# Low key parts with half zeros: a 128-row second score matmul in a decoder trunk on one core

## The chip, the core and the metric

The kernel runs on one core of one Trainium2 chip. The metric is the device time of one execution in microseconds (us): the median of several runs. Five engines of the core appear below: TensorE (PE, with its weight loads as PEld), VectorE (DVE), ScalarE (ACT), GpSimd (POOL) and SyncE (SP), which issues most DMAs.

## The reference

Two layers of a decoder trunk on 512 tokens of width 1024: a norm, one input projection, two attention branches (differential attention with rotary embedding; stick-breaking attention), projections merged under sigmoid gates, an output projection, then a gated FFN of 2816. The change touches the scores alone, which both branches compute per head of 64 features:

```python
def probs(qb, k):                      # differential attention, two maps per head
    sc = jnp.einsum('bhqd,bhkd->bhqk', qb, k).astype(jnp.float32) * scale
    sc = jnp.where(mask, sc, -jnp.inf)
    return jax.nn.softmax(sc, axis=-1)
...
z = jnp.einsum('bhqd,bhkd->bhqk', qb, k).astype(jnp.float32) * scale   # stick-breaking
log_beta = jax.nn.log_sigmoid(z)
log_rem = jnp.where(mask, jax.nn.log_sigmoid(-z), 0.0)
after = lax.cumsum(log_rem, axis=key_axis, reverse=True) - log_rem
a = jnp.where(mask, jnp.exp(log_beta + after), 0.0)
```

## The kernel before

Everything lies with features on partitions. A float32 value is held as a high part in a rounded format (fp32r) and a low part, the rest; a product is high x high, high x low and low x high, in three passes of TensorE. Weights come in chunks of 128x1024 by SyncE's queue, are split by ScalarE (L111) and VectorE or GpSimd (L113), and feed 8 times three matmuls of 128x512 (L204 to L206).

A layer's attention is cut into 8 units: four pairs of stick-breaking heads ("s"), then four differential heads ("d"). A unit has two score maps, c = 0 and 1, each of 64 features: rows 0 to 63 and 64 to 127 of the unit's q and k. A map's scores are cut by query block of 128 tokens, and since later keys are masked, block by block 128, 256, 384 or 512 keys are computed (`SEG`). With heads of 64 features, two of the three passes fit one matmul: `stack_k` lays the high part of a key into both halves of a 128-row tile (`ka`, `kb`), `stack_q` lays high and low part of the query into the two halves (`qa`, `qb`), and one 128-row matmul does high x high and low x high (L397). The third pass, query high times key low, is a matmul of 64 rows: `kl` holds the low parts of both keys, one in each half, and the matmul takes the half of its map from `kl` and from the query tile (L398). There are 2 layers x 16 maps x 4 blocks = 128 of these.

After a map's scores come, for "s", two sigmoids (ACT L427, L429), a mask (POOL L433), a scan (DVE L435) and a product (POOL L437), for "d" a masked softmax (L473 to L489); then transposes on TensorE (L411), the split of their result (ACT L414, DVE L415) and the product with the values (L448, L449 for "s", L504 to L506 for "d"). `LAG` puts two maps between the scores and the product; projections of the next units and of the gates fill TensorE in between (`FILL`).

The program is written unit by unit; a scheduler then sets each engine's order from its own estimate of times. Tiles come from pools: tag `stk` has 8 buffers in turn for `ka`, `kb`, `kl`, `qa`, `qb`, and a new tile of a tag waits until the old one in its buffer has been read. Later gates take `stk` buffers too (`gate_group`). Engines work through their own queue in order, so a waiting instruction holds up those behind it.

Of the kernel before, what the change touches and what calls it, by code (L numbers as in the profile page):

```python
# [24 lines left out]

# score segments of a head: query block -> (bank, column in bank, column in SBUF, keys)
SEG = {0: (0, 0, 0, 128), 2: (0, 128, 128, 384), 3: (1, 0, 512, 512), 1: (2, 0, 1024, 256)}
BANKS = ((0, 512), (512, 512), (1024, 256))
# transposed probabilities: key block -> (bank, column in bank, column in SBUF)
TSEG = {0: (0, 0, 0), 1: (1, 0, 512), 3: (1, 384, 896), 2: (2, 0, 1024)}  # L30
# columns of the packed parameters
C_NA, C_NF, C_NL, C_BG, C_SL, C_LP = 0, 16, 32, 40, 72, 74

# buffers per tag, in the attention pools and of PSUM banks
BUFS = dict(mx=4, sm=4, blk=12, tmp=5, stk=8, v=3, wk=4, wT=3)
BANK_BUFS = dict(mm=3, at=5)
W_BUFS, W_AHEAD = 4, 2
GATES_IN_BLK = 4
FILL = (3, 3, 3, 3, 4, 4, 4, 4)  # projection groups issued under each pair of score maps
LAG = 2  # maps between the scores of a map and its product with the values  # L40


def f32(ap):
    return ap.bitcast(F32)
# [3 lines left out]
def trunk(ctx: ExitStack, tc, xT, par, tab, scn, msk, w_in, w_o, w_out, w_fi, w_fo, out):  # L48
# [9 lines left out]

# [1 line left out]
    UNITS = [("s", i) for i in range(4)] + [("d", i) for i in range(4)]  # L60
# [35 lines left out]
    def w_pieces(*steps):  # L96
        """Loads the next weight chunk and splits it, piece by piece."""
        n = state["next"]
        state["next"] = n + 1
        src = w_src(stream[n])  # L100
        cols = src.shape[1]
        raw = wp.tile([P, 1024], F32, name=f"wr{n}", tag="wr", bufs=2)
        hi = wp.tile([P, 1024], F32R, name=f"wh{n}", tag="wh", bufs=W_BUFS)
        lo = wp.tile([P, 1024], F32R, name=f"wl{n}", tag="wl", bufs=W_BUFS)
        ready.append((stream[n], hi, lo))
        at = 0
        for n_cols in steps:
            c = slice(at, min(at + n_cols, cols))
            at = c.stop
            nc.sync.dma_start(out=raw[:, c], in_=src[:, c])  # L110
            nc.scalar.copy(out=hi[:, c], in_=raw[:, c])  # L111
            eng = nc.gpsimd if stream[n][1] == "in" and n % 4 == 0 else nc.vector
            eng.tensor_tensor(out=lo[:, c], in0=raw[:, c], in1=f32(hi[:, c]), op=ALU.subtract)  # L113
            yield
# [11 lines left out]

# [1 line left out]
    pt = cst.tile([P, C_LP], F32, name="pt")  # L128
# [9 lines left out]

    # the array's clock comes up while the first loads are under way
    warm = bank("mm", "warm")  # L140
    for i in range(9):
        nc.tensor.matmul(warm[:, :P], ones_d, ones_d, start=True, stop=True)

# [1 line left out]
    xs = []  # L145
# [3 lines left out]
    def rsqrt_of(make, ms, name):  # L149
        """1/sqrt(ms + eps) over a PSUM bank: exp(-ln/2), then a Newton step."""  # L150
        y, t = make(f"y{name}"), make(f"t{name}")
        nc.scalar.activation(out=y, in_=ms, func=AF.Ln, bias=eps[:, 0:1])
        state["exp"] = nc.scalar.activation(out=y, in_=y, func=AF.Exp, scale=-0.5)
        nc.vector.scalar_tensor_tensor(out=t, in0=y, scalar=-0.5, in1=y, op0=ALU.mult, op1=ALU.mult)
        nc.vector.scalar_tensor_tensor(out=t, in0=ms, scalar=EPS, in1=t, op0=ALU.add, op1=ALU.mult)
        nc.vector.scalar_tensor_tensor(out=y, in0=t, scalar=1.5, in1=y, op0=ALU.add, op1=ALU.mult)
        return y

    class Norm:
        """Collects a norm as the tiles of x arrive: x*g in two parts, and the mean square."""  # L160

# [32 lines left out]
    def mm(dst, key, rhs, first=True, last=True):  # L194
        """dst += W^T rhs over the k tiles of one weight chunk, three exact passes each."""
        hi, lo = w_get(*key)
        mm_tiles(dst, hi, lo, rhs, first, last)
# [10 lines left out]
    def table(name, after=None):  # L208
        """Loads an activation table set once the work that needs the one before is issued."""
        if after is None:  # L210
            return nc.scalar.preload_act_table_set(name)
        with tc.issue_after(after.ins):
            return nc.scalar.preload_act_table_set(name)
# [25 lines left out]
    for l in range(DEPTH):  # L239
        nc.vector.tensor_tensor(out=lpp[:, l], in0=lpt[:, l, :, 0], in1=lpt[:, l, :, 1], op=ALU.mult)  # L240
        nc.vector.tensor_reduce(out=lps[:, l], in_=lpp[:, l], axis=AX.X, op=ALU.add)
        nc.scalar.activation(out=lps[:, l], in_=lps[:, l], func=AF.Exp)
        li = 0.8 - 0.6 * math.exp(-0.3 * l)
        # the negated weight of the second map
        nc.vector.scalar_tensor_tensor(out=lam[:, l:l + 1], in0=lps[:, l, 1:2], scalar=-li,
                                       in1=lps[:, l, 0:1], op0=ALU.add, op1=ALU.subtract)
        nc.vector.tensor_scalar(out=gsub[:, l:l + 1], in0=pt[:, C_SL + l:C_SL + l + 1],
                                scalar1=1.0 - li, scalar2=None, op0=ALU.mult)
# [14 lines left out]
    for l in range(DEPTH):  # L263
        h = nrm.h
        with ExitStack() as ac:
# [22 lines left out]
            nc.vector.tensor_tensor(out=cs[:, 1], in0=cs[:, 1], in1=r, op=ALU.mult)  # L288

            gates = {}  # L290
            pair = [None]
            TAIL = list(TAIL0)

            def gate_group(key):
# [4 lines left out]
                if n < GATES_IN_BLK:  # L299
                    t = blk(f"gt{j}")  # L300
                elif n < GATES_IN_BLK + BUFS["stk"]:
                    t = T("stk", f"gt{j}")
                else:
                    q = (n - GATES_IN_BLK - BUFS["stk"]) % 2
                    if q == 0:
                        pair[0] = T("wk", f"gt{j}", (P, 1280))
                    t = pair[0][:, q * S:q * S + S]
# [3 lines left out]
            class Unit:  # L311
                """A pair of score maps: two stick-breaking heads, or the two maps of a diff head."""

# [38 lines left out]
                def stack_k(self, t):  # L352
                    ka, kb, kl = self.stk("ka"), self.stk("kb"), self.stk("kl")
                    nc.scalar.copy(out=ka[0:64], in_=t[0:64])
                    nc.scalar.copy(out=kb[64:128], in_=t[64:128])
                    nc.vector.tensor_copy(out=ka[64:128], in_=t[0:64])
                    nc.vector.tensor_copy(out=kb[0:64], in_=t[64:128])
                    nc.vector.tensor_tensor(out=kl[0:64], in0=t[0:64], in1=f32(ka[0:64]), op=ALU.subtract)
                    nc.vector.tensor_tensor(out=kl[64:128], in0=t[64:128], in1=f32(kb[64:128]), op=ALU.subtract)
                    self.k = (ka, kb, kl)  # L360
# [27 lines left out]
                def scores(self, c):  # L388
                    ka, kl = self.k[c], self.k[2]
                    qs = self.q[c]  # L390
                    hs = slice(c * 64, c * 64 + 64)
                    bs = [bank("at", f"s{self.n}{c}{i}_{l}") for i in range(3)]
                    for qb in (0, 2, 3, 1):
# [3 lines left out]
                        nc.tensor.matmul(dst, qs[:, qc], ka[:, 0:n], start=True, stop=False)  # L397
                        nc.tensor.matmul(dst, qs[hs, qc], kl[hs, 0:n], start=False, stop=True)  # L398
                    return bs

                def transposed(self, w, name):
                    """w (queries on partitions) -> its two parts with keys on partitions."""
                    bs = [bank("at", f"t{name}{i}_{l}") for i in range(3)]
# [15 lines left out]
            class SB(Unit):  # L419
                def maps(self, c):  # L420
                    name = f"{self.n}{c}"
                    bs = self.scores(c)
                    # a[k] = beta[k] * prod of (1 - beta[j]) over k < j < q, beta = sigmoid(score / 8)
                    e = T("wk", "e" + name, (P, 1280))
# [6 lines left out]
                    for o in (0, 384, 896, 1152):  # L431
                        d = z[:, o:o + P]
                        nc.gpsimd.tensor_tensor(out=d, in0=d, in1=mk[:, 1], op=ALU.mult)  # L433
                    # masked keys hold the product at one, which also starts each segment afresh
                    nc.vector.tensor_tensor_scan(out=e[:, ::-1], data0=e[:, ::-1], data1=msc[:, ::-1], initial=1.0,  # L435
# [126 lines left out]

# [1 line left out]
            def parts(t, hi, lo):  # L564
# [37 lines left out]
        with ExitStack() as fc:  # L602
# [31 lines left out]
            if last:  # L634
                # the last tile by halves of the tokens: the first half is normed and stored under the second
                w7 = [w_get(l, "fo", 7, c) for c in range(3)]
# [21 lines left out]

# [1 line left out]
def _tiles(np, w, kt, nt):  # L660
    """(L, kt*128, nt*128) -> (L, nt, 128, kt*128): one output tile's weights together."""
    L = w.shape[0]
# [49 lines left out]
```

## Time and profile before

| | |
|---|---|
| median of 3 runs | 1550.02 us (1549.92 to 1557.08) |
| profiled execution, first to last instruction | 1546.8 us |
| the rest of it, by the median | 3.2 us |
| PE busy | 1519.6 us (98%), 6756 matmuls |
| PEld busy | 1229.7 us |
| DVE / ACT / POOL busy | 868.5 / 613.6 / 401.2 us |
| layer 0, attention | about 20 to 300 us |
| layer 1, attention | about 767 to 1080 us |

A busy time adds up the durations of an engine's instructions, and matmuls overlap one another, so PE at 98% does not say that it is at its peak. The chain that ended last is followed back from the last instruction to whatever released each step: it tells where a shorter time would shorten the end. A granted clock of 1.00 is TensorE's 2.4 GHz level, 0.50 its 1.2 GHz level.

### The profile page before, as it was taken

The page shows a single profiled execution, that of the slowest core. Times are in us where ns is not written, and L with a number is a line of the kernel's source. Part 1 is how long each engine was busy: PE and PEld are TensorE (multiplying, and loading weights), DVE is VectorE, ACT ScalarE, POOL GpSimd, SP SyncE. Part 2 cuts the span into 40 slices and gives each one's busy share as a digit, 9 for nine tenths or more (in the row PEclk, how much of TensorE's full clock was granted, in tenths as well). Part 3 has the DMA queues.
Part 4 walks back from the last instruction along what each step waited for, and adds up shares of the span by engine and source line. Part 5 has one row for each costly group of instructions (what it writes and reads, how often), then busy time and mean ns, then how long its engine had stood idle before and what let it go on. Part 6 is the DMA issues. An engine that isn't in the chain of part 4 may idle for free.

```text
span 1546.8 us, 17367 instructions
## 1 busy us (share of the span) xinstructions
PE 1519.6 (98%) x6756; PEld 1229.7 (79%) x6756; DVE 868.5 (56%) x1070; ACT 613.6 (40%) x968; POOL 401.2 (26%) x280
## 2 busy tenths in 40 slices
PE   8999999999999999999998999999999999999997
PEld 6777777888888888888876777778888888888886
DVE  5978867575544545433366778664755444544223
ACT  5655454453422222322254545535433322223221
POOL 3777543001111111100147755410011111111011
PEclk9999999999999999999998989999999999999999
DMA  6122232233323232333321222322322323233331
GB/s 209 65 69 75 69 101 70 82 96 96 96 95 97 95 105 93 95 99 90 119 69 55 61 60 85 96 68 69 109 96 95 96 96 101 94 105 90 98 96 59
DMA packets 43618, 139.58 MB, mean 90 GB/s; under 512 B 5648, under 2 KB 8080, under 8 KB 43536
## 3 DMA queue, kind: packets, MB, share of 16 engines
q1 hardware_dynamic: 42240, 137.38, 28.4%
q8 instruction: 53, 0.87, 0.2%
q10 hardware_dynamic: 1296, 1.09, 0.2%
q14 instruction: 29, 0.24, 0.0%
HBM read 132.16 MB, written 2.10 MB: 87 GB/s over the span
## 4 chain that ended last, share of the span: by engine, by line
PE 88%; DVE 5%; issue 2%; ACT 2%; POOL 1%; DMA 1%; SPq 1%; DVEq 0%; POOLq 0%; ACTq 0%
PE fg L204 5%; PE fu L204 5%; PE fg L205 5%; PE fu L205 5%; PE fu L206 5%; PE fg L206 5%; PE fo L204 5%; PE fo L206 5%; PE fo L205 5%; PE pg L204 4%; PE pg L205 4%; PE pg L206 4%; PE pd L204 2%; PE pd L205 2%; PE pd L206 2%; PE wo L205 2%
## 5 line engine op out<-in xcount | busy, mean ns | idle before, releaser
L111 ACT CAST wh<-wr 128x1024 fp32r<-128x1024 f32 (+3 forms) x251 | 258.0, 1029 | 627.0 <-PE fu L206 160.8
L113 DVE TENSOR_TENSOR wl<-wr,wh 128x1024 fp32r<-128x1024 f32 (+2 forms) x229 | 325.9, 1424 | 205.2 <-ACT wh L111 204.9
L617 POOL TENSOR_TENSOR u<-u,g 128x512 f32<-128x512 f32 x44 | 56.8, 1292 | 441.5 <-DVE u L616 394.3
L205 PE MATMUL fo<-ah,wl 128*128 128x512 f32 (+1 forms) x374 | 141.0, 377 | 0.0
L204 PE MATMUL fo<-ah,wh 128*128 128x512 f32 (+1 forms) x374 | 141.0, 377 | 0.0
L206 PE MATMUL fo<-al,wh 128*128 128x512 f32 (+1 forms) x374 | 140.8, 376 | 0.0
L204 PE MATMUL fg<-hhf,wh 128*128 128x512 f32 x352 | 137.7, 391 | 0.0
L206 PE MATMUL fu<-hlf,wh 128*128 128x512 f32 x352 | 136.9, 389 | 0.0
L205 PE MATMUL fg<-hhf,wl 128*128 128x512 f32 x352 | 136.9, 389 | 0.0
L206 PE MATMUL fg<-hlf,wh 128*128 128x512 f32 x352 | 136.9, 389 | 0.0
L204 PE MATMUL fu<-hhf,wh 128*128 128x512 f32 x352 | 136.9, 389 | 0.0
L205 PE MATMUL fu<-hhf,wl 128*128 128x512 f32 x352 | 136.9, 389 | 0.0
L616 DVE TENSOR_TENSOR u<-fu,yf 128x512 f32<-128x512 f32 x44 | 30.4, 691 | 129.5 <-PE fu L206 129.5
L204 PE MATMUL pg<-hha,wh 128*128 128x512 f32 x256 | 101.6, 397 | 0.0
L205 PE MATMUL pg<-hha,wl 128*128 128x512 f32 x256 | 100.7, 393 | 0.0
L206 PE MATMUL pg<-hla,wh 128*128 128x512 f32 x256 | 100.7, 393 | 0.0
L205 PEld LDWEIGHTS fo<-ah,wl 128*128 128x128 f32 x374 | 70.4, 188 | 13.1
L206 PEld LDWEIGHTS fo<-al,wh 128*128 128x128 f32 x374 | 70.4, 188 | 12.9
L204 PEld LDWEIGHTS fo<-ah,wh 128*128 128x128 f32 x374 | 70.4, 188 | 12.7
L113 POOL TENSOR_TENSOR wl<-wr,wh 128x1024 fp32r<-128x1024 f32 (+3 forms) x22 | 48.7, 2212 | 114.4 <-ACT wh L111 93.1
L204 PE MATMUL pd<-hha,wh 128*128 128x512 f32 x192 | 78.2, 408 | 0.0
L205 PE MATMUL pd<-hha,wl 128*128 128x512 f32 x192 | 78.1, 407 | 0.0
(265 smaller groups left out, 3133.6 us busy)
## 6 DMA issues: line engine op xcount, KB each, us to landing
wr<-in_w_fi_dram SPq DMA_DIRECT2D x88, 512.0 KB, 3.5
wr<-in_w_in_dram SPq DMA_DIRECT2D x78, 512.0 KB, 3.6
wr<-in_w_fo_dram SPq DMA_DIRECT2D x32, 512.0 KB, 3.6
wr<-in_w_o_dram SPq DMA_DIRECT2D x16, 512.0 KB, 3.5
wr<-in_w_out_dram SPq DMA_DIRECT2D x16, 512.0 KB, 3.5
wr<-in_w_fo_dram SPq DMA_DIRECT2D x16, 384.0 KB, 3.2
x<-in_xT_dram SPq DMA_DIRECT2D x8, 256.0 KB, 5.5
cs<-in_tab_dram SPq DMA_DIRECT2D x2, 512.0 KB, 5.3
```

Source lines behind the costliest of these rows:

```text
L111: nc.scalar.copy(out=hi[:, c], in_=raw[:, c])
L113: eng.tensor_tensor(out=lo[:, c], in0=raw[:, c], in1=f32(hi[:, c]), op=ALU.subtract)
L204: nc.tensor.matmul(dst, hi[:, c], rh, start=first and k == 0, stop=False)
L205: nc.tensor.matmul(dst, lo[:, c], rh, start=False, stop=False)
L206: nc.tensor.matmul(dst, hi[:, c], rl, start=False, stop=last and k == n - 1)
L616: nc.vector.tensor_tensor(out=u, in0=bu, in1=r, op=ALU.mult)
L617: nc.gpsimd.tensor_tensor(out=u, in0=u, in1=g, op=ALU.mult)
```

## The change

The low parts of the two keys of a unit get a tile of 128 rows each, `klz[set][c]`. Map 0's low part lies in rows 0 to 63 of the one, map 1's in rows 64 to 127 of the other, and the other half of each is zero. The second score matmul then takes the whole query tile and the whole `klz` tile: the rows that hold the query's low part meet zeros. Four such tiles (two sets, taken in turn by units) are made per layer, and GpSimd writes the zero halves once per layer. `stk` goes from 8 to 6 buffers, and two of the later gates take the tiles of set 0. Comments and blank lines aside, this is all:

```diff
-BUFS = dict(mx=4, sm=4, blk=12, tmp=5, stk=8, v=3, wk=4, wT=3)
+BUFS = dict(mx=4, sm=4, blk=12, tmp=5, stk=6, v=3, wk=4, wT=3)
...
+            klz = [[T(f"klz{b}{c}", f"klz{b}{c}", dt=F32R) for c in range(2)] for b in range(2)]
+            for b in range(2):
+                for c in range(2):
+                    nc.gpsimd.memset(f32(klz[b][c])[64 - 64 * c:128 - 64 * c], 0.0)
...
                 elif n < GATES_IN_BLK + BUFS["stk"]:
                     t = T("stk", f"gt{j}")
+                elif n < GATES_IN_BLK + BUFS["stk"] + 2:
+                    t = T(f"klz0{n - GATES_IN_BLK - BUFS['stk']}", f"gt{j}")
...
                 def stack_k(self, t):
-                    ka, kb, kl = self.stk("ka"), self.stk("kb"), self.stk("kl")
+                    ka, kb = self.stk("ka"), self.stk("kb")
+                    kl = klz[UNITS.index((self.kind, self.i)) % 2]
...
-                    nc.vector.tensor_tensor(out=kl[0:64], in0=t[0:64], in1=f32(ka[0:64]), op=ALU.subtract)
-                    nc.vector.tensor_tensor(out=kl[64:128], in0=t[64:128], in1=f32(kb[64:128]), op=ALU.subtract)
+                    nc.vector.tensor_tensor(out=kl[0][0:64], in0=t[0:64], in1=f32(ka[0:64]), op=ALU.subtract)
+                    nc.vector.tensor_tensor(out=kl[1][64:128], in0=t[64:128], in1=f32(kb[64:128]), op=ALU.subtract)
...
                 def scores(self, c):
-                    ka, kl = self.k[c], self.k[2]
+                    ka, kl = self.k[c], self.k[2][c]
                     qs = self.q[c]
-                    hs = slice(c * 64, c * 64 + 64)
...
                         nc.tensor.matmul(dst, qs[:, qc], ka[:, 0:n], start=True, stop=False)
-                        nc.tensor.matmul(dst, qs[hs, qc], kl[hs, 0:n], start=False, stop=True)
+                        nc.tensor.matmul(dst, qs[:, qc], kl[:, 0:n], start=False, stop=True)
```

Lines behind the new ones carry higher numbers in the changed kernel: the score matmuls are L405 and L406 there, the transposes L419, the products with the values L456 and L457.

In layer 1 the order is kept. TensorE at the scores of its last unit, before (`sd` is the score bank, `kad` and `kbd` the high parts, `kld` the low parts):

```order
L397 MATMUL sd_1_7689<-kad_1_7471,qad_1_7522 128x128
L398 MATMUL sd_1_7689<-kld_1_7473,qad_1_7522 128x128
L397 MATMUL sd_1_7689<-kad_1_7471,qad_1_7522 128x384
L398 MATMUL sd_1_7689<-kld_1_7473,qad_1_7522 128x384
L397 MATMUL sd_1_7690<-kad_1_7471,qad_1_7522 128x512
```

And the same place after:

```order
L405 MATMUL sd_1_7689<-kad_1_7472,qad_1_7522 128x128
L406 MATMUL sd_1_7689<-klz_1_5869,qad_1_7522 128x128
L405 MATMUL sd_1_7689<-kad_1_7472,qad_1_7522 128x384
L406 MATMUL sd_1_7689<-klz_1_5869,qad_1_7522 128x384
L405 MATMUL sd_1_7690<-kad_1_7472,qad_1_7522 128x512
```

Nothing moved there; only the low part comes from a tile of its own.

In layer 0 the order of all engines differs. TensorE at the first product with the values of that layer, before (`ts` are the transposes of the first map, `avs_0_615` its product with the values: `ths` the high, `tls` the low part):

```order
L411 MATMUL ts_0_595<-ident,zs_0_365 128x128 x4
L411 MATMUL ts_0_596<-ident,zs_0_365 128x128 x2
L448 MATMUL avs_0_615<-ths_0_597,vs_0_348 128x512
L397 MATMUL ss_0_666<-kbs_0_412,qbs_0_454 128x128
L449 MATMUL avs_0_615<-tls_0_598,vs_0_348 128x512
L398 MATMUL ss_0_666<-kls_0_413,qbs_0_454 128x128
```

And after:

```order
L419 MATMUL ts_0_601<-ident,zs_0_372 128x128 x2
L204 MATMUL ps_0_796<-hha_124,wh_634 128x512
...
L456 MATMUL avs_0_620<-ths_0_602,vs_0_355 128x512
L405 MATMUL ss_0_671<-kbs_0_419,qbs_0_460 128x128
L406 MATMUL ss_0_671<-klz_0_325,qbs_0_460 128x128
L405 MATMUL ss_0_671<-kbs_0_419,qbs_0_460 128x384
L457 MATMUL avs_0_620<-tls_0_603,vs_0_355 128x512
```

Three projection matmuls (`ps`) and two more score matmuls now stand between the last transposes and the product that needs the low part `tls`.

GpSimd at the start of layer 0, after (`acca` is the sum of squares of the norm, `wl` the low part of a weight chunk, `qas` the query tile of the first unit):

```order
L187 TENSOR_TENSOR acca_102<-acca_102,sqa_183 128x512
L294 MEMSET klz_0_322 64x512
L294 MEMSET klz_0_323 64x512
L294 MEMSET klz_0_324 64x512
L294 MEMSET klz_0_325 64x512
L113 TENSOR_TENSOR wl_229<-wr_227,wh_228 128x1024
L113 TENSOR_TENSOR wl_561<-wr_559,wh_560 128x1024
L375 TENSOR_TENSOR qas_0_342<-qns_0_340,qas_0_342 64x512
```

Before, the weight split stood right behind the sum of squares; the four memsets have come between the two.

## Rows read from the trace of the kernel before

**Rows 1.** The page's chain that ended last, share by engine.

```profile
PE 88%; DVE 5%; issue 2%; ACT 2%; POOL 1%; DMA 1%; SPq 1%; DVEq 0%; POOLq 0%; ACTq 0%
```

**Rows 2.** Timeline of TensorE, layer 0: start us, duration us, line, tiles, rows*columns, form.

```profile
216.09 0.38 PE L398 MATMUL sd<-kld,qad 64*128 64x256 f32 x1
216.40 0.33 PE L397 MATMUL sd<-kbd,qbd 128*128 128x128 f32 x1
216.66 0.33 PE L398 MATMUL sd<-kld,qbd 64*128 64x128 f32 x1
216.91 0.44 PE L397 MATMUL sd<-kbd,qbd 128*128 128x384 f32 x1
217.28 0.44 PE L398 MATMUL sd<-kld,qbd 64*128 64x384 f32 x1
217.65 0.50 PE L204 MATMUL pd<-hha,wh 128*128 128x512 f32 x1
```

**Rows 3.** Timeline of TensorE, layer 1, a product with the values, all rows full.

```profile
1010.78 0.33 PE L504 MATMUL avd<-thd,vd 128*128 128x384 f32 x1
1010.95 0.34 PE L505 MATMUL avd<-tld,vd 128*128 128x384 f32 x1
...
1011.43 0.28 PE L505 MATMUL avd<-tld,vd 128*128 128x256 f32 x1
1011.54 0.29 PE L506 MATMUL avd<-thd,vd 128*128 128x256 f32 x1
...
1011.73 0.28 PE L505 MATMUL avd<-tld,vd 128*128 128x128 f32 x1
1011.84 0.27 PE L506 MATMUL avd<-thd,vd 128*128 128x128 f32 x1
```

**Rows 4.** L398 by stretch: length, busy (xcount) of PE and PEld, clock, DMA.

```profile
40.00:78.50 38.50, 4.66 (x12) 2.12 (x12) 0.96 0.17 55
108.60:137.50 28.90, 4.15 (x10) 1.77 (x10) 1.00 0.25 73
137.50:300.00 162.50, 13.47 (x33) 6.03 (x33) 1.00 0.25 79
780.70:830.90 50.20, 4.83 (x14) 2.30 (x14) 0.99 0.23 74
887.20:926.60 39.40, 4.02 (x8) 1.77 (x8) 0.87 0.18 54
926.60:1080.00 153.40, 11.69 (x28) 5.22 (x28) 0.98 0.26 81
```

**Rows 5.** Chain's shares from 62.7, 108.6, 780.7 and 887.2 us on, as the text says.

```profile
by line: DVE es L435 46.2%; issue 16.3%; DVE wl L113 11.7%; DVE kas L356 5.4%; DVE kls L358 5.3%; DVE vs L384 4.7%; DVE tls L415 3.9%; DVE kbs L357 3.6%; DVE qns L321 3.0%; DVE kls L359 0.2%
...
by line: DVE es L435 23.2%; issue 17.0%; DMA knd0s<-knd0u 6.9%; POOL zs L433 6.4%; POOL knd L334 6.2%; POOL knd0u L329 6.1%; SPq L333 6.1%; DVE kld L359 5.8%; DVE tls L415 4.8%; ACT es L427 4.8%; ACT zs L429 3.4%; DVE kad L356 2.4%; DVE kbd
...
by line: issue 12.8%; POOL zs L433 10.4%; DVE kls L359 10.4%; DMA wr<-in_w_in_dram 8.8%; ACT wh L111 8.2%; DVE wl L113 7.7%; DVE kls L358 6.6%; DVE kas L356 5.0%; POOL zs L437 4.8%; POOL qbs L367 4.3%; POOL qas L366 2.6%; ACT qas L364 2.5%;
...
by line: issue 14.3%; DMA qnd0s<-qnd0u 9.5%; DVE wl L113 9.4%; SPq L333 8.9%; DMA knd1s<-knd1u 8.2%; DVE kld L358 6.6%; DVE kbd L357 6.4%; DVE kld L359 4.3%; DVE tls L415 4.2%; DVE qnd L330 3.9%; ACT ths L414 3.4%; POOL knd L334 3.3%; POOL 
```

**Rows 6.** Stretches: length, busy of PE, PEld, DVE, ACT, POOL, then clock, DMA.

```profile
830.00:840.00 10.00, 9.05 (x22) 6.56 (x23) 6.69 (x8) 4.43 (x9) 6.97 (x6) 0.50 0.18 52
...
1021.20:1024.60 3.40, 3.40 (x8) 2.26 (x9) 2.29 (x7) 0.00 (x0) 0.00 (x0) 0.50 0.47 154
983.70:987.00 3.30, 3.30 (x9) 2.53 (x10) 3.30 (x10) 1.64 (x7) 0.47 (x1) 0.50 0.50 164
```

**Rows 7.** Timeline of TensorE, two waits, in brackets: idle us before, released by.

```profile
78.51 0.50 PE L449 MATMUL avs<-tls,vs 128*128 128x512 f32 x1 [1.15 <-DVE tls L415]
...
830.95 0.79 PE L449 MATMUL avs<-tls,vs 128*128 128x512 f32 x1 [4.40 <-DVE tls L415]
```

**Rows 8.** GpSimd: a memset in the groups by line; a row of its timeline.

```profile
masks.py:197 POOL MEMSET ident<- 128x128 f32 x1 | 0.2, 204 | 0.3 <-POOLq L703 0.3
...
28.64 2.39 POOL L113 TENSOR_TENSOR wl<-wr,wh 128x1024 fp32r<-128x1024 f32 x1 [5.88 <-ACT wh L111]
```

## The prediction

> **What bounds the kernel now.** I read the chain that ended last first: 88% of the span is TensorE, 5% VectorE, everything else 7% [rows 1]. So a microsecond taken from TensorE is worth a microsecond wherever the chain lies on it, and nothing where it does not. The second view is the timeline of TensorE inside a score map, where the change works. The reader should look at starts, not at durations: matmuls overlap, and the time that one takes of the engine is the distance from its start to the next start. In a run of projections and scores of layer 0 [rows 2] the start after the 64-row matmul of 256 columns comes 0.31 us later (216.09 to 216.40), after that of 128 columns 0.25, after that of 384 columns 0.37. The full-row matmuls between them are as slow: 0.26 for 128 columns, 0.37 for 384. Full-row matmuls of the same widths that follow one another, in the product with the values, take 0.17 us for 384 columns, 0.11 for 256 and 0.11 for 128 [rows 3]. They add into one bank just as the score pair does, so it is not the accumulation that costs. What is left is that the number of rows of the array changes, from 128 to 64 or back, and each change costs 0.14 to 0.20 us whatever the width.
>
> Third, the granted clock: in 1021.20 to 1024.60 it is 0.50, the 1.2 GHz level, right behind a stretch of nothing but such scores, and in 830.00 to 840.00 it is 0.50 behind a long wait of TensorE [rows 6].
>
> **The change part by part.**
>
> *Row changes removed.* There are 2 layers x 16 maps x 4 query blocks = 128 low-part matmuls. Two changes of 0.14 to 0.20 us on each, 0.36 us together at the mean of rows 2, would be 46 us. That is too much, since the first change of a run, behind an ordinary projection, is cheaper (about 0.1 us), and some low-part matmuls stand next to each other. I therefore took the same difference over the whole timeline, for each pair of neighbouring matmuls whose row counts differ (248 pairs were recorded, five of them in rows 2): distance of the starts, less the distance that full-row matmuls of that width have. It comes to 40.0 us, 0.31 per low-part matmul. The streamed columns stay as they are: the second matmul reads as many columns as before, half of its rows being zero. So 40.0 us of engine time goes.
>
> *What of it lies on the path.* In four stretches the chain leaves TensorE for 12 us or more at a time [rows 5]: 62.7 to 78.5 (46.2% of it the scan), 108.6 to 137.5, 780.7 to 830.9 and 887.2 to 926.6. There TensorE waits for VectorE, GpSimd or a shuffle by DMA, and arriving earlier only makes it wait longer. I also count the scores from 40 us on as lost, since behind them the same VectorE queue ends at 78.5. By the counts of low-part matmuls [rows 4] 12 + 10 + 14 + 8 = 44 of them lie there: 44 x 0.31 = 13.6 us lost. What is on the path is 40.0 - 13.6 = 26.4 us.
>
> *Clock.* The half-clock stretch of 1021.20 to 1024.60 costs about 1.7 us (half of 3.4), and one of the same length at 983.7 follows the same kind of stretch [rows 6]. Behind neither did the engine wait for data; only the row changes had thinned its work. I take both as gone: 3.4 us. Against that stands the wait at 78.51: today 1.15 us, it would grow by 12 x 0.31 = 3.7 to 4.9, longer than the 4.40 us at 830.95 [rows 7], and that one was followed by 10 us at 0.50, which cost 5 us. I give that an even chance: 2.5 us back. Sum: 26.4 + 3.4 - 2.5 = 27.3 us.
>
> *Zero halves.* Four GpSimd memsets of 64x512 per layer. No row shows one of this size; one of 128x128 takes 0.2 us, and a two-operand operation on 1024 columns takes 2.39 us [rows 8], so half of that, 1.2 us, bounds one of 512 columns from above. Four take 0.8 to 4.8 us. The order puts them in layer 0 between the last sum of squares and a weight split that waits 5.88 us for its data today [rows 8], and in layer 1 just as far ahead of the units, where GpSimd waits long. They are covered: 0. If the cover failed, or VectorE's splits beside them were slowed, 0 to 2 us in layer 0; that goes into the range.
>
> *Key stacking.* The two subtractions write two tiles instead of two halves of one, with the same shape: 0. *Two stack buffers fewer:* a unit now takes four buffers of six instead of five of eight. Counting the rotation through, each k tile still reuses a q or low tile of the unit two before, and each q tile a k tile of the unit before, so no wait is added; the low parts alternate between two sets, again two units apart. The gates find the same number of places. All 0.
>
> *Order.* In layer 1 all engines keep their order but for the memsets. In layer 0 the scheduler has moved projections, scores and the products with the values against each other. TensorE's first product with a low part (the wait at 78.51) now has three projections, a product and three scores between it and the last transposes, where a product and one score stood; elsewhere such a cover shrinks by as much. I take 0 with 5 us to either side, the size of the largest wait of rows 7.
>
> **The rivals.** *The other engines eat more of it.* If VectorE's queue ends every map of the stick-breaking half, only the scores from 137.5 to 300 and from 926.6 to 1080 count: 33 + 28 = 61 [rows 4], 61 x 0.31 = 18.9, less 2.5 for the clock: 1533.6 us. For it: in both layers the chain leaves TensorE early in that half. Against it: in 78.5 to 108.6 and 830.9 to 887.2 it is TensorE again.
>
> *All of it arrives.* The waits shrink with their inputs, since the chains through VectorE begin at a score: 40.0 + 3.4 = 43.4, so 1506.6 us. Against it: the stretch from 780.7 begins at the norm, not at a score.
>
> *The gap stays.* It is 0.14 to 0.20 us long, and one weight load is 0.18 us (2.12 us for 12 in rows 4). Were it a weight load that could not run under the matmul before, full-row scores would pay it too: 1550, with up to 2 us of memsets 1552. Against it stand rows 3: there full-row loads are hidden, at 0.17 us for 384 columns. The Trainium skill, on the page "TensorE: Matmul & The Clock Gate", Part 3, says that a weight load overlaps a running matmul only where the row groups differ; by that rule the new pair, both on all rows, would keep the gap and the time would be this rival's. The trace does not agree: the 0.17 us of rows 3 leave no room for a load of 0.18 us beside the streaming.
>
> *Slower.* The new order of layer 0 puts a consumer on TensorE's queue too early, as at 830.95: such a place costs 4.40 us of wait and 5 us of half clock, 9.4 together. It decides from three such places on (28 us); with four the time is 1550.0 - 27.3 + 37.6 = 1560.3 us. Against it: the distances from a map's scores to its transposes, counted in matmuls, are much as they were in either layer.
>
> **How the numbers follow.** The profiled execution's span is 1546.8 us, 3.2 under the median 1550.02 of the timed runs; I take the 3.2 as unchanged. 1550.0 - 27.3 = 1522.7, so 1523 us. Chances: the forecast 0.60, other engines eat more 0.18, all of it 0.12, the gap stays 0.05, slower 0.05. The range leaves out the last two and reaches from all of it, 1507, to the first rival with the order against it, 1533.6 + 5, with the memsets 1540. 0.5% of the time, about what a measurement of this kernel can tell from no change, is 7.8 us. Faster by more than that: 0.60 + 0.18 + 0.12 = 0.90. Within it: 0.05. Slower: 0.05.
>
> **What would show it.** In the profile after, the low-part matmuls should read 128*128, and within a map the starts should lie 0.11, 0.11 to 0.13, 0.17 and 0.23 us apart; a 128-column pair still 0.25 apart would show the third rival. Layer 1, where the order did not change, is the clean place: from 926.6 to 1080 it should get shorter by 28 x 0.31 + 3.4 = 12 us, while 780.7 to 830.9 should hardly move and its waits grow by 4 us. The clock should be full behind the last scores of layer 1. If the wait at 78.51 does not grow, the first stretch was not bound as I read it, and more of the 13.6 us arrives; if layer 0 gains much less than layer 1, the new order is the place to look.

## The result, and the profile after

The changed kernel takes 1536.49 us (median of 4 runs, 1535.02 to 1538.29), the kernel before beside it 1551.79 (4 runs, 1549.92 to 1557.08). The ratio is 0.9889, with a 95% interval of 0.9862 to 0.9916: 17 us faster by the ratio (15 by the two medians), where 27 were forecast. The time lies in the range that was given; some ten of the 27 us are missing.

The page of the changed kernel, its busy times and the chain that ended last by engine:

```profile
PE 1482.3 (96%) x6756; PEld 1228.0 (80%) x6756; DVE 873.2 (57%) x1070; ACT 611.3 (40%) x968; POOL 412.6 (27%) x288
...
PE 79%; DVE 8%; POOL 5%; issue 3%; ACT 2%; DMA 1%; SPq 1%; DVEq 0%; POOLq 0%; ACTq 0%
```

TensorE has the same 6756 matmuls and is 37 us less busy; its share of the chain has fallen from 88% [rows 1] to 79%, and most of what it gave up went to VectorE (5% to 8%) and GpSimd (1% to 5%). The scores of layer 0 in the same unit as [rows 2], in the timeline of the changed kernel (start us, duration us, line, tiles, rows*columns, form):

```profile
219.56 0.22 PE L405 MATMUL sd<-kad,qad 128*128 128x128 f32 x1
219.62 0.27 PE L406 MATMUL sd<-klz,qad 128*128 128x128 f32 x1
219.73 0.39 PE L405 MATMUL sd<-kad,qad 128*128 128x384 f32 x1
219.96 0.34 PE L406 MATMUL sd<-klz,qad 128*128 128x384 f32 x1
220.14 0.39 PE L405 MATMUL sd<-kad,qad 128*128 128x512 f32 x1
220.37 0.40 PE L406 MATMUL sd<-klz,qad 128*128 128x512 f32 x1
220.60 0.28 PE L405 MATMUL sd<-kad,qad 128*128 128x256 f32 x1
220.73 0.28 PE L406 MATMUL sd<-klz,qad 128*128 128x256 f32 x1
220.84 0.22 PE L405 MATMUL sd<-kbd,qbd 128*128 128x128 f32 x1
```

Behind the low-part matmuls (L406) the next start comes 0.11, 0.18, 0.23 and 0.11 us later, for 128, 384, 512 and 256 columns. The gaps are gone to the last one; so something else took ten microseconds. It is in one layer. Counted from a layer's first projection (`p`) to the first matmul of the branch projections (`ws`), in one trace of each kernel:

| us | layer 0 | layer 1 | gaps at row changes, layer 0 / 1 | waits of TensorE over 0.3 us | time at half clock |
|---|---|---|---|---|---|
| before | 313.8 | 321.0 | 20.0 / 20.0 | 2.5 / 9.0 | 3.4 / 27.3 |
| after | 317.1 | 307.6 | 0 / 0 | 17.1 / 22.3 | 23.9 / 13.7 |

A gap is the distance of two starts with different row counts, less the distance that full-row matmuls of that width have. Waits and half clock of layer 0 are counted from its first scores on. Everything outside the two attentions is the same to 0.5 us. Layer 1, whose order did not change, got 13.4 us shorter; layer 0, whose order did, got 3.3 us longer although the same 20 us of gaps left it. In layer 1 the sum closes: 20.0 us of gaps less 13.3 of longer waits, and half of the 13.6 us fewer at half clock, give 13.5.

Where layer 0 lost it is in TensorE's timeline of the changed kernel; in brackets the idle us before a matmul and what ended it:

```profile
72.33 0.48 PE L419 MATMUL ts<-ident,zs 128*128 128x128 f32 x1 [4.64 <-POOL zs L445]
...
100.60 0.30 PE L405 MATMUL ss<-kas,qas 128*128 128x128 f32 x1 [1.86 <-DVE vs L393]
...
137.90 0.33 PE L405 MATMUL ss<-kbs,qbs 128*128 128x128 f32 x1 [2.04 <-DVE os L462]
...
165.71 0.48 PE L419 MATMUL ts<-ident,zs 128*128 128x128 f32 x1 [2.69 <-DVE os L462]
...
199.45 0.51 PE L405 MATMUL sd<-kbd,qbd 128*128 128x512 f32 x1 [2.12 <-DVE os L462]
...
223.78 0.80 PE L204 MATMUL pd<-hha,wh 128*128 128x512 f32 x1 [1.97 <-ACT knd3s L336]
```

Before, the layer had three waits over 0.3 us from its first scores on, 1.15 the longest [rows 7]. And at the end of each of the last five waits, or within half a microsecond of it, the clock is at half, as the stretches of the changed kernel show (length, busy of PE, PEld, DVE, ACT, POOL, then clock, DMA):

```profile
100.80:104.20 3.40, 3.35 (x12) 3.03 (x12) 2.91 (x5) 0.56 (x1) 0.00 (x0) 0.50 0.00 0
138.40:141.80 3.40, 3.40 (x10) 2.71 (x10) 3.40 (x3) 3.12 (x7) 3.32 (x3) 0.50 0.00 0
165.70:169.10 3.40, 3.39 (x11) 2.71 (x12) 1.91 (x4) 2.02 (x8) 0.00 (x0) 0.50 0.00 0
199.80:203.20 3.40, 3.40 (x11) 2.72 (x10) 2.50 (x9) 2.89 (x10) 0.46 (x1) 0.50 0.00 0
223.70:227.10 3.40, 3.32 (x8) 2.64 (x9) 3.36 (x7) 1.96 (x8) 1.31 (x1) 0.50 0.50 154
```

A stretch of 3.40 us at half clock costs half of its length, 1.7. With its wait, each of these five places costs 3.6 to 4.4 us, where TensorE is what the rest waits for.

### The profile page after: what moved, and what is told of

Read it like the earlier page. It is cut to its first block, busy times and chain, and to the rows that moved or that the text cites. A ratio compares the mean times of both kernels' runs of the same rounds, so it can differ in the third digit from the quotient of the medians.

```text
span 1536.5 us, 17374 instructions
## 1 busy us (share of the span) xinstructions
PE 1482.3 (96%) x6756; PEld 1228.0 (80%) x6756; DVE 873.2 (57%) x1070; ACT 611.3 (40%) x968; POOL 412.6 (27%) x288
## 4 chain that ended last, share of the span: by engine, by line
PE 79%; DVE 8%; POOL 5%; issue 3%; ACT 2%; DMA 1%; SPq 1%; DVEq 0%; POOLq 0%; ACTq 0%
PE fg L204 5%; PE fu L204 5%; PE fg L205 5%; PE fu L205 5%; PE fu L206 5%; PE fg L206 5%; PE fo L204 5%; PE fo L206 5%; PE fo L205 5%; PE pg L206 3%; PE pg L205 3%; PE pg L204 3%; PE wo L205 2%; PE wo L206 2%; PE wo L204 2%
## 5 line engine op out<-in xcount | busy, mean ns | idle before, releaser
L187 POOL TENSOR_TENSOR accf<-accf,sqf 128x512 f32<-128x512 f32 x10 | 18.5, 1846 | 220.0 <-ACT sqf L185 220.0
```

Of the source, the lines that this page charges most:

```text
L187: eng.tensor_tensor(out=self.acc, in0=self.acc, in1=sq, op=ALU.add)
```

## The experiments

Two explanations stood against each other. *Order*: the pair of full rows is worth what was forecast, and layer 0's new order takes part of it back. *Others*: the other engines cannot deliver faster, whatever the order, so the gain would be about 17 us in any order. The order of a whole layer is a scheduler's answer to small changes of the code: with two of the four zero halves per layer written by VectorE, or all four, it comes out as in the kernel before on every engine, the memsets aside. So rows and order can be set apart.

### 64 rows in the new order

The changed kernel with the second matmul back at 64 rows; order, tiles and buffers as in the changed kernel:

```diff
-nc.tensor.matmul(dst, qs[:, qc], kl[:, 0:n], start=False, stop=True)
+nc.tensor.matmul(dst, qs[c * 64:c * 64 + 64, qc], kl[c * 64:c * 64 + 64, 0:n], start=False, stop=True)
```

> The changed kernel with only the second score matmul put back to 64 rows (it takes its map's half of the query tile and of klz); memsets, tiles, buffers and the order of every engine are those of the changed kernel. Theory 'order': layer 0's new order is itself worse and ate the gain there, so this kernel is slower than the kernel before, about 1562 us (1557 to 1568), with layer 0 longer by 5 to 15 us and layer 1 as in the kernel before. Theory 'others': the order is neutral and VectorE and GpSimd hold layer 0 back whatever TensorE does; then it lies within 4 us of the kernel before, 1548 to 1556.

Measured: 1560.45 us (1558.16 to 1563.03), ratio 1.0042, 1.0026 to 1.0059. Without the full rows the rest of the change is a small loss, as *order* expected. Layer 0 takes 322.6 us in its trace, 8.8 more than before, and layer 1 324.6, 3.6 more; the second figure, in an unchanged order, says how far single executions differ.

### 128 rows in the order of before

The changed kernel with the zero halves written by VectorE:

```diff
-nc.gpsimd.memset(f32(klz[b][c])[64 - 64 * c:128 - 64 * c], 0.0)
+nc.vector.memset(f32(klz[b][c])[64 - 64 * c:128 - 64 * c], 0.0)
```

> The changed kernel with the zero halves written by VectorE instead of GpSimd. Nothing else is edited, but with that the scheduler gives TensorE, VectorE, ScalarE and GpSimd exactly the order of the kernel before in both layers, the memsets aside. Theory 'order': the gain arrives in layer 0 as well, about as much as the 13.4 us of layer 1: 1526 us (1521 to 1531). Theory 'others': layer 0 gains nothing in this order either: 1537 us (1533 to 1541).

Measured: 1522.45 us (1521.68 to 1525.53), ratio 0.9801, 0.9786 to 0.9817. *Others* is out: the same matmuls in the order of before gain nearly twice as much. Its layer 0 takes 301.0 us, 12.8 less than before, its layer 1 306.8, 14.2 less.

### Fewer changes of the row count, without new tiles

The kernel before with the matmuls of a map's scores in groups, so that low parts of several query blocks follow one another; 146 neighbours with different row counts are recorded in place of 248 (`low` takes the place of the fixed pair, `start` and `stop` follow it):

```diff
-for qb in (0, 2, 3, 1):
+for qb, low in ((0, 0), (0, 1), (2, 1), (3, 1), (1, 1), (2, 0), (3, 0), (1, 0)):
```

> The kernel before with the eight score matmuls of a map in another order: high and low part of block 0, then the low parts of blocks 2, 3 and 1, then their high parts, so that 64-row matmuls stand together; the program has 146 changes of the row count instead of 248. The scheduler moves other work with it. If the price is per change of row count, the starts inside a run of 64-row matmuls are as close as those of full rows (0.17 us for 384 columns, 0.11 for 128) and the sum of the gaps falls from 40 to about 23 us; the time falls by up to 17 us, as far as the order lets it, some 1541 us. If a 64-row matmul is slow by itself, the starts inside such a run stay 0.2 us further apart and the sum stays at 40 or more.

Measured: 1539.16 us (1535.76 to 1542.13), ratio 0.9907, 0.9884 to 0.9930. Gaps of 16 to 21 us are left in its trace, by the distance that is taken for full rows, where before had 39 to 44. The scheduler answered this edit, too, with another order on every engine, in both layers, so the time is that of rows and order together; what the experiment shows stands in the starts. The timeline of TensorE in this kernel, equal tiles in one row (x4: four matmuls):

```profile
215.37 0.22 PE L401 MATMUL sd<-kad,qad 128*128 128x128 f32 x1
215.52 0.89 PE L399 MATMUL sd<-kld,qad 64*128 64x128 f32 x4
216.34 0.79 PE L401 MATMUL sd<-kad,qad 128*128 128x384 f32 x3
```

Four 64-row matmuls of 128, 384, 512 and 256 columns take 0.82 us from the first start to the next full-row start. At the distances of full rows they would take 0.11 + 0.17 + 0.23 + 0.11 = 0.62. So a run of 64-row matmuls pays 0.20 us once (and 0.09 at its start, 0.15 where full rows of 128 columns had 0.06 above). It is the change that costs, not the 64 rows; no zero half is needed to show it.

### Tiles and buffers alone

The second experiment's kernel with the second matmul at 64 rows: what is left of the change is tiles, memsets and six stack buffers in place of eight.

```diff
-nc.gpsimd.memset(f32(klz[b][c])[64 - 64 * c:128 - 64 * c], 0.0)
+nc.vector.memset(f32(klz[b][c])[64 - 64 * c:128 - 64 * c], 0.0)
...
-nc.tensor.matmul(dst, qs[:, qc], kl[:, 0:n], start=False, stop=True)
+nc.tensor.matmul(dst, qs[c * 64:c * 64 + 64, qc], kl[c * 64:c * 64 + 64, 0:n], start=False, stop=True)
```

> The new tiles, six stack buffers, memsets on VectorE and the order of the kernel before on every engine, but the second score matmul back at 64 rows: what is left of the change is tiles and buffers alone. Theory 'rows and order' (the whole gain is the row changes, the loss is the order of layer 0; tiles, memsets and buffers cost nothing): as the kernel before, 1553 us, 1550 to 1556, ratio 0.998 to 1.002, with 248 changes of the row count and gaps of 40 us in the trace. Theory 'buffers' (six stack buffers or a tile of its own for the low parts let work start earlier, and part of the gain of e2 is theirs): 1535 to 1547 us. If two buffers fewer hold something up: above 1557 us.

Measured: 1554.76 us (1546.95 to 1559.24, 10 runs), ratio 1.0005, 0.9987 to 1.0023: nothing that can be measured. With it the square of rows and order is complete, as ratios to the kernel before, which was timed anew beside each group of runs:

| | order of before | new order of layer 0 | price of the order |
|---|---|---|---|
| 64 rows | 1.0005 | 1.0042 | 0.4%, 6 us |
| 128 rows | 0.9801 | 0.9889 | 0.9%, 14 us |
| worth of full rows | 2.0%, 32 us | 1.5%, 24 us | |

The two don't simply add: the order costs more once TensorE is early. The intervals of the four ratios, 0.2 to 0.3% to either side, leave this difference just clear of the noise. The traces say where it comes from. With 64 rows the new order has 5.3 us of waits and 13.7 us at half clock in layer 0, the order of before 3.8 and 6.8; the 1.5 us of waits and half of the 6.9 us make 4.9 of the 5.5 us by which layer 0 is longer (322.6 against 317.1). Of the five waits shown for the changed kernel two stand there already, in the timeline of the first experiment; the other three came with the full rows:

```profile
164.71 0.33 PE L419 MATMUL ts<-ident,zs 128*128 128x128 f32 x1 [1.25 <-DVE os L462]
...
224.86 0.79 PE L204 MATMUL pd<-hha,wh 128*128 128x512 f32 x1 [1.97 <-ACT knd3s L336]
```

### Two of the four memsets on GpSimd

```diff
-nc.gpsimd.memset(f32(klz[b][c])[64 - 64 * c:128 - 64 * c], 0.0)
+(nc.vector if b else nc.gpsimd).memset(f32(klz[b][c])[64 - 64 * c:128 - 64 * c], 0.0)
```

> The change with 128 rows, the zero halves of set 0 written by GpSimd and those of set 1 by VectorE; apart from these memsets every engine keeps the order of the kernel before. Theory 'order': as e2, 1522.5 us, 1520.5 to 1524.5, since memsets are covered on either engine. Theory 'memsets' (GpSimd's memsets hold up the first weight splits of a layer, and that is what the changed kernel pays in layer 0): two of four stand on GpSimd, so half of its 16 us: 1530 us, 1528 to 1533.

Measured: 1522.49 us (1520.27 to 1525.34), ratio 0.9799, 0.9772 to 0.9825. It is the second experiment's time to 0.1 us, with two memsets per layer on GpSimd, so it is not GpSimd's work on the memsets that layer 0 pays for. In the changed kernel the memsets read (duration min/median/max in ns, first and last start):

```profile
L294 POOL MEMSET klz<- x8: 517/520/524, 22.8 to 771.0; 64x512 f32 x8
```

This kernel has the order of before and two GpSimd memsets per layer, so it is the best to lay beside the changed one. All its waits of TensorE over 0.6 us in layer 0 from 40 us on, and one long stretch (columns as above):

```profile
73.95 0.30 PE L419 MATMUL ts<-ident,zs 128*128 128x128 f32 x1 [2.58 <-DVE vs L393]
...
76.42 0.41 PE L419 MATMUL ts<-ident,zs 128*128 128x128 f32 x1 [1.84 <-ACT zs L437]
...
130.11 0.50 PE L457 MATMUL avs<-tls,vs 128*128 128x512 f32 x1 [2.44 <-DVE tls L423]
...
226.98 0.33 PE L382 MATMUL vtd<-ident,vnd 128*128 128x128 f32 x1 [1.99 <-DVE vnd L329]
```

```profile
134.60:320.00 185.40, 182.77 (x889) 153.38 (x888) 135.06 (x227) 99.05 (x188) 66.86 (x45) 1.00 0.27 84
```

From 134.6 us on the clock is full here, where the changed kernel has four half-clock stretches behind four waits. Three of those waits end with `os` (L462), VectorE's last step of a product with the values, which sets its PSUM bank free. That line in the trace of the changed kernel (duration ns, first and last start, who waited how many us and times), and then in this kernel's:

```profile
L462 DVE TENSOR_TENSOR os<-avs,os x8: 671/688/695, 90.4 to 198.7; 64x512 f32<-64x512 f32 x8
...
who waited for it (us, times):
...
  PE ts L419: 2.7, 1
...
  PE sd L405: 2.1, 1
  PE ss L405: 2.0, 1
```

```profile
L462 DVE TENSOR_TENSOR os<-avs,os x8: 673/689/696, 85.4 to 177.2; 64x512 f32<-64x512 f32 x8
```

In this kernel nobody waited for it, and the last of the eight starts at 177.2 us, against 198.7. Why it is late at 137.15 is seen in VectorE's timeline, the changed kernel first and then this one: in the changed kernel a key's stacking and a scan of 2.97 us stand right ahead of it, in this one the scan comes behind it.

```profile
132.41 0.83 DVE L367 TENSOR_TENSOR klz<-knd,kad 64x512 fp32r<-64x512 f32 x1
133.28 0.84 DVE L368 TENSOR_TENSOR klz<-knd,kbd 64x512 fp32r<-64x512 f32 x1
134.15 2.97 DVE L443 TENSOR_TENSOR_SCAN es<-es,msc 128x1280 f32<-128x1280 f32 x1
137.15 0.69 DVE L462 TENSOR_TENSOR os<-avs,os 64x512 f32<-64x512 f32 x1
...
136.87 0.68 DVE L462 TENSOR_TENSOR os<-avs,os 64x512 f32<-64x512 f32 x1
137.47 2.81 DVE L443 TENSOR_TENSOR_SCAN es<-es,msc 128x1280 f32<-128x1280 f32 x1
```

At the other two, 164.96 and 198.70, it is a key's stacking (L367, L368) and the masks and maxima of a softmax (L481, L482) that stand ahead.

### 64 rows in layer 0 alone

The second experiment's kernel (memsets on VectorE) with one line more changed:

```diff
-nc.tensor.matmul(dst, qs[:, qc], kl[:, 0:n], start=False, stop=True)
+hs = slice(c * 64, c * 64 + 64) if l == 0 else slice(0, P)
+nc.tensor.matmul(dst, qs[hs, qc], kl[hs, 0:n], start=False, stop=True)
```

> As e2 (order of the kernel before, memsets on VectorE), but in layer 0 the second score matmul is at 64 rows again, in layer 1 it stays at 128. Theory 'independent layers' (e2's trace: layer 0 gains 12.8 us, layer 1 14.2 us): the gain of layer 0 goes, 1522.5 + 12.8 = 1535.3 us, 1533 to 1538, with 124 changes of the row count in layer 0 and none in layer 1. Theory 'the tail takes it' (what layer 0 gains is given back in layer 1): nearer to e2, 1523 to 1528 us.

Measured: 1536.50 us (1535.47 to 1537.52), ratio 0.9883, 0.9864 to 0.9902. So layer 0's rows are worth 13 us (to 0.9800) and layer 1's 19 (from 1.0005); nothing is given back between the layers. One trace now has both forms of the same code. Timeline of TensorE in this kernel, layer 0 and then layer 1:

```profile
216.69 0.38 PE L407 MATMUL sd<-klz,qad 64*128 64x256 f32 x1
217.00 0.33 PE L405 MATMUL sd<-kbd,qbd 128*128 128x128 f32 x1
217.25 0.33 PE L407 MATMUL sd<-klz,qbd 64*128 64x128 f32 x1
217.51 0.44 PE L405 MATMUL sd<-kbd,qbd 128*128 128x384 f32 x1
...
1010.33 0.28 PE L407 MATMUL sd<-klz,qad 128*128 128x256 f32 x1
1010.44 0.22 PE L405 MATMUL sd<-kbd,qbd 128*128 128x128 f32 x1
1010.50 0.27 PE L407 MATMUL sd<-klz,qbd 128*128 128x128 f32 x1
1010.61 0.39 PE L405 MATMUL sd<-kbd,qbd 128*128 128x384 f32 x1
```

The three distances are 0.31, 0.25 and 0.26 us in the one and 0.11, 0.06 and 0.11 in the other.

## Why the prediction was right or wrong

**Direction and range held, one term did not.** The forecast of 1523 is within 1 us of the change in an unchanged order (1522.45 and 1522.49); the changed kernel is 14 us above that. That it still lies in the range is luck as far as the mechanism goes: the upper end was drawn for the first rival, in which the other engines eat more, and it was the order that filled the room. The step that failed is *Order*: "I take 0 with 5 us to either side, the size of the largest wait of rows 7." It measured 14 us by the ratios, and 16 in the traces (317.1 against 301.0 or 301.2). What was wrong in it is the count: it looked for one wait, at one place, and gave a bound for that one. The new order moved VectorE's queue as well as TensorE's, and the loss came in instalments: from 100 us on it has five waits of some 2 us, each with a half-clock stretch, where the kernel with two GpSimd memsets has two, and one stretch. By the traces, waits are 7.7 us longer than in the kernel with two GpSimd memsets (17.1 against 9.4), and 17.1 more us run at half clock (23.9 against 6.8), which is 8.5 lost: 16.2 together, for 15.9. That these two carry the loss is an accounting of traces; no run took one of them away alone, nor does a run say which of the moved rows matters most.

**Row changes removed: 40.0 us.** Held. The total leans on the distance taken for full rows, since 128 columns take 0.06 or 0.11 us in the rows above, by their place: 39 to 44 us before, 16 to 21 with 146 changes, 0 with none.

**What lies on the path.** The size held, as nearly as one execution tells. In the order of before, TensorE's waits grew by 12 to 13 us against the kernel with new tiles and 64 rows, and by 19 against the execution shown before; 13.6 were forecast as lost. Against that same execution the time at half clock fell by 3 to 10 us, worth 2 to 5, where the forecast had 0.9 for the clock; so part of the good sum is two misses that offset each other. Layer 1 of the changed kernel shows the places: its first wait for a low part ended 65.4 us after the layer's first matmul before (830.95 of [rows 7], less 765.53), and as long, within 0.1 us, after:

```profile
768.99 0.39 PE L204 MATMUL p<-hha,wh 128*128 128x512 f32 x1
...
834.54 0.69 PE L457 MATMUL avs<-tls,vs 128*128 128x512 f32 x1 [3.77 <-DVE tls L423]
...
925.25 0.80 PE L456 MATMUL avs<-ths,vs 128*128 128x512 f32 x1 [5.49 <-ACT pd L487]
```

So that stretch did not move, as forecast; its waits over 0.3 us grew by 2.4 us, not by 4, and 3.4 us of it, from 821.0 on, ran at half clock. All of the layer's gain came behind it: 4.9 us up to the wait at 925.25 and 8.5 from there on, where 12 were forecast for the last part. The wait of 5.49 was not foreseen, and half clock from 923.4 to 930.3 goes with it. It is not the full rows that make it: the two kernels with new tiles and 64 rows wait 4.87 and 4.64 us at that place.

**Clock.** The half-clock stretches behind the last scores of layer 1 are gone, as forecast: from 930.3 to the end of that attention it is full. That the full rows did it is not shown. Of the kernels with 64 rows and new tiles, the one in the new order has two such stretches there (3.4 us at 994.4, 6.8 at 1032.0, no wait over 0.3 us near them); the one in the order of before has none, its one stretch there, at 1011.8, comes with a wait of 2.77. The even chance on the first product came out in between in the order of before: at the transposes ahead of it, waits of 2.58 and 1.84, 4.4 together where 4.9 was forecast, and 3.4 us at half clock in 76.5 to 79.9 (6.8 in the second experiment), not 10. In the new order the wait stands at the transposes (4.64 at 72.33) and the product waits only 0.86.

**Zero halves, stacking, buffers: 0.** Held. The fourth experiment has tiles, buffers and memsets alone, at 1.0005, but with the memsets on VectorE. On GpSimd a memset takes 0.52 us, against the bounds of 0.2 and 1.2, and they are covered: the weight split behind them starts at 28.52 us, and at 28.64 before [rows 8].

**3.2 us around the span.** Wrong: the span of a run and its time lie 1.8 us apart in all runs here, so the execution of [rows 1] to [rows 8] took 1548.6 us, some 5 under the median that the kernel before had later (1553.4 of 8 runs, 1553.8 of 13). Against these medians 31 us were gained in the order of before, between the traces 27 to 28; the rest fits that the execution of [rows 1] to [rows 8] was one of the shorter ones of its kernel. So the forecast's gain, 27.3, fell short of the 31, and that 1523 is hit to 1 us is in part luck: its starting point, 1550.0, lay 3 to 4 us under the later medians.

**The rivals.** *The other engines eat more* came near the time (1533.6) by another mechanism: in the order of before they don't. *All of it arrives* is out: 31 of its 43.4 us came even in the order of before. *The gap stays* is out: the weight loads take as long as ever in the groups of the changed kernel (ns of one behind the busy time) and no gap is left beside them.

```profile
L406 PEld LDWEIGHTS sd<-klz,qad 128*128 128x128 f32 x32 | 6.0, 189 | 0.7
```

The Trainium skill's rule on the page "TensorE: Matmul & The Clock Gate", Part 3, that a load overlaps a running matmul only where the row groups differ, does not hold for this pair: both use all rows, and starts 0.06 to 0.18 us apart leave no room for 0.189. The same part of the Trainium skill also says that a load into a background weight buffer is pulled ahead; no run here tells whether that is what happens.

*Slower* had the right mechanism, a consumer that the new order puts too early, and the wrong size: it counted places of 9.4 us each, three of them to use up the gain; five of some 4 us went with a loss of nearly half of it. What came too late at three of the five was the release of a bank, not the low part that rival thought of.

## What to carry to other kernels

Where matmuls of 64 and 128 rows take turns, price every change of the row count at 0.14 to 0.20 us, and either fill the small ones up with zeros or put them next to each other; the second needs no tile, and here, with the order that came with it, gave 0.9% where the zeros gave 2.0% in the order of before. Where a scheduler sets the order, compare the orders before the times: here four memsets per layer of 0.52 us on one engine and not on another decided over 14 us. A new order is not worth "0 with a bound for one wait"; go through each bank's release and each key's stacking on VectorE's queue, and count the places.

## What the runs showed of the hardware

- A change between 64 and 128 rows costs TensorE 0.16 us at the mean (40.0 us over 248 in the kernel before), and inside a run of 64-row matmuls there is none to be seen (four of them take 0.82 us, 0.62 and one change). On the Trainium skill's page "TensorEngine Tiling (Array Packing)", Key Properties, a change of the tiling mode drains TensorE; the trace agrees, if 64 rows among 128 are such a mode, and gives it this price. That the time goes into a drain is seen in no row.
- Waits of only 1.86 to 2.69 us each came with 3.4 us at 0.50; before, the wait of 4.40 had 10 us of it [rows 6, 7]. Others as long had none: behind 226.98 in the fifth experiment (1.99 us) the clock is full.
- In the kernel before, two neighbouring 64-row matmuls on different halves of the rows (`ss<-kls,qas` of 384 columns and `ss<-kls,qbs` of 128, layer 1) start 0.01 us apart, at 798.82 and 798.83; the fourth experiment has the same pair 0.01 apart. Low parts of the two maps side by side would be another way to spend less on them; no run tried it.
